# A tiny load ahead of the first big one in a streaming row-sum kernel

## The chip, the cores and the metric

The kernel runs on one core of one Trainium2 chip. The metric is the device time of one execution in microseconds (us); lower is better. The time given is the median of several runs of the same program. A profile of one execution shows what each engine did: DVE is the vector engine, ACT the scalar engine, POOL the GpSimd engine, and SP the sync engine, which here only issues DMA transfers (SPq in the profile is its instruction queue).

## The reference

```python
def setup_inputs():
    batch, seq, dim = 32, 512, 1024
    return {"x": np.random.randn(batch, seq, dim).astype(np.float32)}

def reference(x):
    relu_x = np.maximum(x, 0)
    return np.sum(relu_x, axis=-1).astype(np.float32)
```

The input is 16384 rows of 1024 float32 values, 67.1 MB in all. Each row is clamped below at zero and summed; the output is 16384 sums, 64 KB.

## The kernel before, in words

The rows are seen as 128 partitions of 128 rows. A block is 16 rows on each of the 128 partitions, 8 MB, so there are eight blocks. Block 0 is taken from the first 2048 rows (its source is contiguous, 64 KB for each partition); blocks 1 to 7 share the other 14336 rows, 112 for each partition, so their 64 KB runs lie 448 KB apart.

Three buffers `io0` to `io2`, each 64 KB for each partition, take the blocks in turn. All transfers are issued by SP, in the order of the program, and go into one DMA queue. `load` (L97 to L104, the transfer itself at L99) issues a transfer with a semaphore of its own; from block 3 on it first waits on the DVE semaphore until the block that held the buffer before has been summed. The seven blocks 0 to 6 are whole transfers of 8 MB. The last block is cut into six: 8 rows, 4 rows, then 4 rows in four pieces (1164, 642, 120 and 122 KB), so that little work is left when the last bytes land. The two last pieces go to small tiles `piece0` and `piece1`.

ACT clamps a block in place (`clamp`, L117) once its load's semaphore stands at 16; DVE then sums it (`total`, L125). In blocks 5 and 6 and in the tail single rows are clamped and summed by one instruction, on ACT (`act_row`, L132) or on DVE (`dve_row`, L140, and the last one at L224). Sums go to the tile `res`. Three stores (`store`, L109 waits for ACT, L110 issues the transfer and waits for DVE) write `res` to the output: block 0's sums, the rest but two columns, and the last two columns. At the very end SP clears the semaphores (L46) and waits until the stores have landed (L47).

The program has an opening block, in which the engines do their own setup (POOL writes four constants), and then a body. `open_without_barrier` takes the barrier out of the opening block and moves the first `EARLY` instructions of SP's body to the front of SP's part of the opening block; it asserts that they are transfers:

```python
    loads = [i for i in body if i.engine == SP][:n_loads]
    for i in loads:
        assert isinstance(i, mybir.InstDMACopy)
        body.remove(i)
    at = next(n for n, i in enumerate(opening) if i.engine == SP)
    opening[at:at] = loads
```

With `EARLY = 1` block 0's load is SP's first instruction. SP then branches to the body and issues the loads of blocks 1 and 2, without a wait.

Of the kernel before, what the change touches and what calls it, by code (L numbers as in the profile page):

```python
# [4 lines left out]
F32 = mybir.dt.float32  # L5
RELU = mybir.ActivationFunctionType.Relu
MAX, ADD = mybir.AluOpType.max, mybir.AluOpType.add
P = 128
# [5 lines left out]
TWO = [[16], [16], [16], [8, 8], [8, 8], [7, 7], []]  # L14
# [5 lines left out]
TAIL = [8, 4]  # L20
START_PIECE, END_PIECE = 280, 260
PIECES = [240, 244]

EARLY = 1


def kernel(tc: tile.TileContext, x: bass.AP, out: bass.AP):
    nc = tc.nc
    sems = Semaphores(tc)

    tc.close()
    tc.compile()
    nc.cur_bb = nc.bb_map[tc.start_bb_name]
    body = nc.cur_bb.bb.instructions
    ends = list(body)
    body.clear()
    n_stores = relu_sum(nc, sems, x, out)
    body.extend(ends)


    nc.cur_bb = nc.bb_map[tc.start_bb_name + "_end"]
    nc.cur_bb.bb.instructions.clear()
    nums = sorted(s.num for s in (*sems.loads, sems.act, sems.dve))
    cleared = range(nums[0], nums[-1] + 1)
    assert len(cleared) == len(nums)
    nc.sync.sem_clear(cleared)  # L46
    nc.sync.wait_ge(sems.stored, 16 * n_stores).then_inc(sems.stored, -16 * n_stores)  # L47
    open_without_barrier(tc, EARLY)


class Semaphores:
    def __init__(self, tc: tile.TileContext):
        n = len(TWO) + len(TAIL) + 2 + len(PIECES)
        self.loads = [tc.alloc_semaphore(f"load{i}") for i in range(n)]
        self.act = tc.alloc_semaphore("act")
        self.dve = tc.alloc_semaphore("dve")
        self.stored = tc.alloc_semaphore("stored")


def relu_sum(nc, sems: Semaphores, x: bass.AP, out: bass.AP):  # L60
    x_flat = x.flatten_outer_dims()
# [4 lines left out]
    assert sum(TAIL) == ROWS - 4 and START_PIECE + END_PIECE + sum(PIECES) == D  # L66

    bufs = [nc.alloc_sbuf_tensor(f"io{i}", [P, ROWS, D], F32) for i in range(NBUF)]
    res = nc.alloc_sbuf_tensor("res", [P, NT], F32)

    extra = len(PIECES) + 1
# [18 lines left out]
    def sums(m, n):  # L90
        if m < ROWS:
            return of[:, m : m + n], res[:, m : m + n]
        return ov[:, m - ROWS : m - ROWS + n], res[:, m : m + n]
# [3 lines left out]
    def load(dst, src, after=None):  # L97
        nonlocal n_load
        dma = nc.sync.dma_start(out=dst, in_=src)  # L99
        if after:  # L100
            dma.wait_op(sems.dve, after[1], "sem-ge")
        dma.then_inc(sems.loads[n_load], 16)
        n_load += 1
        return sems.loads[n_load - 1]  # L104

    def store(m, n, act, dve):
        nonlocal n_store
        dst, src = sums(m, n)
        nc.sync.wait_ge(sems.act, act)  # L109
        nc.sync.dma_start(out=dst, in_=src).wait_op(sems.dve, dve, "sem-ge").then_inc(  # L110
            sems.stored, 16
        )
        n_store += 1
# [24 lines left out]
    def dve_row(ap, accum_out, loaded):  # L138
# [12 lines left out]
        i.then_inc(sems.dve, 1)  # L151
        n_dve += 1

    freed = []
    m = 0
    for j in range(NB):
# [58 lines left out]

    store(0, ROWS, *freed[0])
    store(ROWS, NT - ROWS - 2, sums_act, sums_dve)

# [17 lines left out]
def open_without_barrier(tc: tile.TileContext, n_loads: int):  # L238

    SP = mybir.EngineType.SP
    blocks = tc.nc.main_func.blocks
    opening = blocks[0].instructions
    body = next(b for b in blocks if b.name == tc.start_bb_name).instructions
    for i in list(opening):
        if isinstance(i, (mybir.InstDrain, mybir.InstEventSemaphore)):
            opening.remove(i)
# [6 lines that stand above are left out]
# [30 lines left out]
```

## Time and profile before

| | |
|---|---|
| median of 3 runs | 161.29 us (161.19 to 161.3) |
| span of the profiled execution, first to last instruction | 159.6 us |
| median less span, work around the program's instructions | 1.7 us |
| DVE busy | 117.6 us (74%) |
| ACT busy | 104.2 us (65%) |
| POOL busy | 0.2 us |
| read from memory, mean rate over the span | 67.11 MB, 421 GB/s |
| packets of the one DMA queue | 2304 |
| SP's first load issued | 0.00 us |
| ACT's first clamp starts | 21.87 us |

How to read it: the page gives no time of the profiled execution other than its span, so the span is set beside the median of the timed runs; what lies around the span is the difference. All times inside the profile count from the first instruction. The packet records of the trace give, for every DMA packet, when it started, how long it took and its size; a load of one block is 128 packets of 64 KB, eight for each of 16 DMA engines.

### The profile page before, as it was taken

How to read it: one execution, taken by the hardware profiler on the slowest of the kernel's cores; microseconds unless marked ns; L12 is line 12 of the kernel's file. 1: busy time of each engine (PE TensorE's matmuls, PEld its weight loads, DVE VectorE, ACT ScalarE, POOL GpSimd, SP SyncE). 2: the span in 40 equal slices, each digit the busy share in tenths (PEclk: the TensorE clock that was granted, in tenths of full speed). 3: DMA queues.
4: the chain of work that ended last, by engine and by line, in shares of the span. 5: the costliest groups of instructions: out<-in, count | busy, mean ns of one | idle time of the engine just before them, and what ended most of it. 6: DMA issues, size and time to landing. Idle time of an engine off the chain costs nothing.

```text
span 159.6 us, 120 instructions
## 1 busy us (share of the span) xinstructions
DVE 117.6 (74%) x43; ACT 104.2 (65%) x50; POOL 0.2 (0%) x4
## 2 busy tenths in 40 slices
DVE  0000000009999499994999999999999999999986
ACT  3000059990699708996099951999329993499995
POOL 0000000000000000000000000000000000000000
DMA  7996996996997999979979969969969969798993
GB/s 279 509 526 263 526 526 263 526 509 279 526 476 312 526 394 394 526 345 443 526 328 460 526 263 526 526 263 526 509 279 526 493 296 526 337 452 382 418 412 119
DMA packets 2304, 67.18 MB, mean 421 GB/s; under 512 B 640, under 2 KB 896, under 8 KB 1024
## 3 DMA queue, kind: packets, MB, share of 16 engines
q1 hardware_dynamic: 2304, 67.18, 98.0%
HBM read 67.11 MB, written 0.07 MB: 421 GB/s over the span
## 4 chain that ended last, share of the span: by engine, by line
DMA 43%; DVE 34%; ACT 17%; another core or an unknown queue 3%; SPq 1%; issue 0%
DMA io<-in_x_dram 43%; DVE res L125 32%; ACT io L117 17%; DVE io L140 1%; SPq L99 1%; DVE piece L224 0%; DVE piece L140 0%
## 5 line engine op out<-in xcount | busy, mean ns | idle before, releaser
L125 DVE TENSOR_REDUCE res<-io 128x8 f32<-128x8192 f32 (+2 forms) x9 | 101.1, 11287 | 40.0 <-ACT io L117 40.0
L117 ACT ACTIVATE io<-io 128x8192 f32<-128x8192 f32 (+2 forms) x9 | 81.7, 9110 | 47.7 <-DMA io<-in_x_dram 47.7
L132 ACT ACTIVATE io<-io 128x1024 f32<-128x1024 f32 x20 | 20.9, 1045 | 6.0 <-DMA io<-in_x_dram 6.0
L140 DVE TENSOR_SCALAR_CACHE_REDUCE io<-io 128x1024 f32<-128x1024 f32 (+2 forms) x15 | 15.8, 1110 | 0.5 <-DMA io<-in_x_dram 0.4
L132 ACT ACTIVATION_READ_ACCUMULATOR io<-io 128x1 f32 x20 | 3.8, 188 | 0.0
L117 ACT ACT_TABLE_LOAD x1 | 1.3, 1283 | 0.1
L140 DVE DVE_READ_ACCUMULATOR io<-io 128x1 f32 x15 | 1.2, 82 | 0.0
L224 DVE TENSOR_SCALAR_CACHE_REDUCE piece<-piece 128x247 f32<-128x247 f32 x1 | 0.4, 410 | 0.0
L140 DVE TENSOR_SCALAR_CACHE_REDUCE piece<-piece 128x240 f32<-128x240 f32 x1 | 0.4, 397 | 0.0
L269 POOL MEMSET const-bfloat16-1.0<- 128x1 bf16 x1 | 0.1, 101 | 0.0
L269 POOL MEMSET const-uint8-127<- 128x1 uint8 x1 | 0.1, 101 | 0.0
L269 POOL MEMSET const-float32-0.0<- 128x1 f32 x1 | 0.1, 98 | 0.2 <-issue 0.2
L269 POOL MEMSET const-float32-1.0<- 128x1 f32 x1 | 0.1, 98 | 0.0
L224 DVE DVE_READ_ACCUMULATOR piece<-piece 128x1 f32 x1 | 0.1, 83 | 0.0
L140 DVE DVE_READ_ACCUMULATOR piece<-piece 128x1 f32 x1 | 0.1, 82 | 0.0
## 6 DMA issues: line engine op xcount, KB each, us to landing
io<-in_x_dram SPq DMA_DIRECT2D x1, 4096.0 KB, 21.6
io<-in_x_dram SPq DMA_DIRECT2D x1, 2048.0 KB, 26.1
io<-in_x_dram SPq DMA_DIRECT2D x1, 1164.0 KB, 28.4
io<-in_x_dram SPq DMA_DIRECT2D x1, 642.0 KB, 29.5
piece<-in_x_dram SPq DMA_DIRECT2D x1, 122.0 KB, 29.2
piece<-in_x_dram SPq DMA_DIRECT2D x1, 120.0 KB, 29.4
io<-in_x_dram SPq DMA_DIRECT2D x7, 26.9
out_dram<-res SPq DMA_DIRECT2D x1, 55.0 KB, 1.6
```

Source lines behind the costliest of these rows:

```text
L99: dma = nc.sync.dma_start(out=dst, in_=src)
L117: i = nc.scalar.activation(out=ap, in_=ap, func=RELU)
L125: nc.vector.tensor_reduce(out=res[:, m : m + n], in_=ap, axis=mybir.AxisListType.X, op=ADD).wait_op(sems.act, n_act, "sem-ge").then_inc(se ...
L132: i = nc.scalar.activation(out=ap, in_=ap, func=RELU, accum_out=accum_out)
L140: i = nc.vector.tensor_scalar(out=ap, in0=ap, scalar1=0.0, scalar2=None, op0=MAX, op1=ADD, accum_out=accum_out,)
L224: nc.vector.tensor_scalar(out=last[:, :], in0=last[:, :], scalar1=0.0, scalar2=None, op0=MAX, op1=ADD, accum_out=res[:, NT - 2 : NT - 1],) ...
L269: nc = _bacc.Bacc("TRN2", target_bir_lowering=False, num_devices=1)
```

## The change

`EARLY` becomes 2 and a new load is put ahead of all others: 8 bytes for each of 16 rows, from the first 16 rows of `x`, into 16 partitions of a new scratch tile `woken`. It has a semaphore of its own. It becomes SP's first instruction and block 0's load the second; both stand ahead of the branch to the body. Nothing reads `woken`; SP waits for the new semaphore once, just ahead of the first store.

```diff
-EARLY = 1
+EARLY = 2
...
-        n = len(TWO) + len(TAIL) + 2 + len(PIECES)
+        n = 1 + len(TWO) + len(TAIL) + 2 + len(PIECES)
...
     bufs = [nc.alloc_sbuf_tensor(f"io{i}", [P, ROWS, D], F32) for i in range(NBUF)]
+    woken = nc.alloc_sbuf_tensor("woken", [P, 2], F32)
     res = nc.alloc_sbuf_tensor("res", [P, NT], F32)
...
+    wake = load(woken[:16, :], x_flat[:16, :2])
     freed = []
...
+    nc.sync.wait_ge(wake, 16)
     store(0, ROWS, *freed[0])
     store(ROWS, NT - ROWS - 2, sums_act, sums_dve)
```

In the built program the scratch tile moves `res`, `piece0` and `piece1` up by 32 bytes in each partition; the three buffers stay where they were. No instruction of ACT, DVE or POOL is added, removed or moved.

## The prediction

> **What bounds the kernel now.** I read the chain that ended last first. From the page and, below it, the end of the same chain in order of time (start, length, what):
>
> ```profile
> DMA 43%; DVE 34%; ACT 17%; another core or an unknown queue 3%; SPq 1%; issue 0%
> ...
> 126.91 28.43 DMA io<-in_x_dram
> 155.34 0.02 issue
> 155.37 2.02 DVE io L140 x6
> 157.39 0.33 DVE piece L140 x2
> 157.72 0.02 issue
> 157.74 0.42 DVE piece L224 x2
> ```
>
> The chain passes through ACT and DVE in the middle, which could be read as a compute bound. The waits and ACT's timeline (start, length, instruction, idle time before it and what ended that) say otherwise:
>
> ```profile
> ACT io L117 <- DMA io<-in_x_dram: 47.7, 6, 20.5
> ...
> 21.87 13.86 ACT L117 ACTIVATE io<-io 128x16384 f32<-128x16384 f32 x1 [20.47 <-DMA io<-in_x_dram]
> 41.19 13.86 ACT L117 ACTIVATE io<-io 128x16384 f32<-128x16384 f32 x1 [5.46 <-DMA io<-in_x_dram]
> 60.55 13.86 ACT L117 ACTIVATE io<-io 128x16384 f32<-128x16384 f32 x1 [5.50 <-DMA io<-in_x_dram]
> 79.90 13.95 ACT L117 ACTIVATE io<-io 128x8192 f32<-128x8192 f32 x2 [5.50 <-DMA io<-in_x_dram]
> ```
>
> ACT starts each block when it lands and then idles some 5.4 us; blocks land every 19.35 us, (79.90 - 41.19)/2. The next view is the queue:
>
> ```profile
> q1 hardware_dynamic: 2304, 67.18, 98.0%
> ...
> SPq L99 <- DVE res L125: 123.3, 5, 51.7
> ```
>
> The queue's packets fill 98.0% of sixteen engines' span. SP does wait for DVE before it issues later blocks, which puts DVE into the chain, but block 3's load is issued at 53.0 us while block 2 lands only at 60.5 us: 7.5 us of stock in the queue. The packet records show the same on every engine: chained by end and start, 64 KB packets take 2.418 us each, with breaks of at most 4 ns from the first packet to the last of the input. So the end is where the slowest DMA engine's first packet ends, plus a fixed amount of streaming, plus a DVE tail that starts on landings. What shifts the stream by d shifts the end by d.
>
> **The start, which is all the change touches.** At 19.35 us a block the first could land at 19.35; ACT starts at 21.87, so the start costs 2.5 us. SP's early timeline:
>
> ```profile
> 0.00 0.86 SPq L99 DMA_DIRECT2D io<-in_x_dram  x2
> ...
> 0.12 1.28 ACT L117 ACT_TABLE_LOAD   x1
> ...
> L99 SPq DMA_DIRECT2D io<-in_x_dram x11: 327/383/442, 0.0 to 127.4; - x11
> ```
>
> The first issue lasts 0.383 us, the second starts at 0.433. By the packet records the sixteen first packets start between 1.014 and 1.810 us (five by 1.05, the last three at 1.52, 1.72 and 1.81) and take 2.50 to 3.27 us instead of 2.418. Start plus excess is the moment from which an engine streams at full rate: 1.55 to 2.17 us. The slowest starts at 1.397, takes 3.187 and ends at 4.584; its offset stays to the end of the input. From its 2.17 us, 0.3 us more lie between a block's last packet and its semaphore (eight packets end at 21.52, the last landing is 21.85).
>
> For comparison, the only transfer onto an empty queue later: the last store is issued at 158.188 to 158.521, its packets start at 159.014 (0.83 us after the issue began, 0.49 after it ended), and the sixteen semaphore packets lie within 0.15 us. The first load needs 0.63 us from issue end to the first packet and 0.80 us from the first engine to the last. So 0.14 us of latency and some 0.65 us of spread may be a first-use cost. Or they may belong to reading 64 KB runs from memory on sixteen engines at once, which a store from on-chip memory does not do. The trace of before cannot tell these apart, and the forecast hangs on it.
>
> **Part by part.**
>
> - *One more issue ahead of block 0.* Price: one issue (0.327 to 0.383 us by the row above) and the 0.04 us gap to the next, so 0.37 to 0.42; nothing hides it, since SP's first instruction starts the span. The program's first issue is the longer one, so I take 0.42.
> - *What the small load gives back.* Lower end nothing: the latency and the spread of block 0 repeat. Next bound 0.14 us: the common latency, if only that is first use. I take half of this, 0.07. The far bound is the rival below.
> - *The small load's own packets.* One 8-byte packet and one semaphore packet for each engine; such packets take 7 to 9 ns in the last store, so 0.02 us, inside the latency of block 0: nothing on the path. If block 0 had to wait until they were confirmed, see the second rival.
> - *Blocks 1 and 2 are issued 0.4 us later*: covered by block 0's 19 us of streaming. The queue's stock of 7.5 us moves along with landings.
> - *The wait ahead of the first store*: one semaphore instruction, 17 ns at L109, on SP at 128.9 us, after the last load's issue. Behind it stand only the stores; SP waits until 156.5 for the second one anyway, 27 us of cover. The new semaphore was raised 125 us earlier.
> - *32 bytes of shift of `res` and the pieces, one more semaphore in the range that is cleared* (a single instruction, 58 ns at the end): nothing. The bound is the pieces' packets, 45 ns each and sixteen for each engine; a tenth more is 0.07 us, kept in the range.
> - *The tail*: DVE's last 2.8 us follow landings and move with them.
>
> Sum: 0.42 - 0.07 = +0.35 us, 161.29 + 0.35 = 161.64 (span 159.6 to 160.0, with the same 1.7 us around it). Ends of this case: 0.37 - 0.14 = +0.23, and 0.42 + 0.07 + 0.1 for a longer issue of block 0 behind a busy issuer (second issues last 0.43 us and more) = +0.6; so 161.5 to 161.9.
>
> The Trainium skill speaks against the change: "DMA: Bandwidth & Descriptors", section "Rules for kernel authors", says that many small transfers should be coalesced, since under 64 KB one pays mostly overhead. By that rule the 128 bytes are pure loss; the row prices the loss at one issue. The same page, "Latency and other measured facts", gives about 0.8 us as the least round trip to memory; put on the path whole, it would make the sum +1.2 us instead of +0.35. No row shows a later packet waiting for such a trip.
>
> **The rivals.**
>
> *The small load takes the slow start on itself (faster).* Place: the sixteen engines between 1.0 and 2.2 us. If the spread is each engine's first use, the small load spends it while SP is still issuing block 0. Its packets start as late as block 0's did (to 1.81), and block 0's follow at once; without excess the slowest ends at 1.81 + 2.42 = 4.23 instead of 4.58: -0.35 us, 160.94. If even the wake is shorter, the floor is the second issue's end, 0.42 + 0.38, plus 0.49 of latency, plus 2.42 = 3.71: -0.87, 160.42. For it: the spread of 0.80 us against 0.15, and the first five engines starting together while eleven trail. Against it: the engine that ends last is not one that starts late; it started at 1.397 and lost 0.77 us inside its packet, and the one that started last lost only 0.08. That looks like sixteen readers held up in common rather than engines asleep, and a read of 8 bytes each does not repeat that load. It decides from the point where the slowest first packet ends before 4.26 us.
>
> *Issue and gain cancel (no change).* The late engines start as before at up to 1.81, the early ones no longer at 1.01 but near 1.3, and the excess stays up to 0.85: 1.3 + 0.85 + 2.42 = 4.57 against 4.58. 161.3, within 0.2% (0.32 us, about what a measurement of this kernel can tell from no change).
>
> *Block 0 waits for the small load's confirmation (slower by more).* Between the last packet and the last semaphore of a load lie 0.3 to 0.4 us. On top of 0.42 that is +0.8: 162.1. Against it: semaphore packets stand between all blocks, and no engine pauses there for more than 4 ns.
>
> That the change doesn't do what it says is excluded by the built order: SP's list begins with the 16x2 load, then block 0, then the branch. Whether the engines are any readier for it is the first rival.
>
> **How the numbers follow.** The forecast (serial cost) 0.46, of which 0.04 falls under +0.32; the fast rival 0.35, of which 0.02 is too small to count; no change 0.14; confirmation 0.05. So faster 0.33, within 0.2% 0.20, slower 0.47. The range must reach into the fast rival: from 160.7, a little beyond the middle of that rival's two prices (160.94 and 160.42), to 161.95, just over the forecast's upper end; left out are the confirmation case and the rest of the fast one, under 2 in 10. The forecast's own range is 161.5 to 161.9.
>
> **What would show it.** Right: SP's first issue 0.33 to 0.38 us, block 0's at about 0.42; first 64 KB packets starting at 1.3 us or later with the old spread; ACT's first clamp at 22.2 instead of 21.87; all later rows shifted by the same 0.35; blocks still 19.35 us apart. Wrong: a first clamp at or before 21.6, with first packets that start within 0.2 us of each other or take close to 2.42 us (fast rival); a clamp at 21.8 to 21.95 (cancelled); or block distances other than 19.35, which would mean that the change reached beyond the start.

## The result, and the profile after

The changed kernel is slower by about what one issue costs: 161.49 us (161.42 to 161.66, 11 runs) against 161.13 us (160.93 to 161.30, 11 runs), a ratio of 1.0025 with a 95% interval of 1.0017 to 1.0034, that is +0.27 to +0.55 us around a difference of 0.36 us. The three runs that were known before are among the eleven.

The page and the end of the chain in order of time, of the changed kernel:

```profile
span 160.1 us, 121 instructions
...
q1 hardware_dynamic: 2336, 67.18, 97.7%
...
DMA 43%; DVE 34%; ACT 17%; another core or an unknown queue 3%; SPq 1%; issue 0%
```

```profile
127.36 28.42 DMA io<-in_x_dram
155.78 0.02 issue
155.81 1.59 DVE io L141 x4
...
158.20 0.42 DVE piece L227 x2
```

There is one instruction more and 32 packets more (a data packet and a semaphore packet for each engine); the chain's shares are the same in whole per cent. The last stretch begins 0.46 us later than before (127.36 against 126.91) and is as long. Everything from the first block on is 0.43 to 0.47 us later, as SP's and ACT's timelines show (start, length, instruction, idle time before it):

```profile
0.00 0.39 SPq L100 DMA_DIRECT2D woken<-in_x_dram  x1
0.44 1.36 SPq L100 DMA_DIRECT2D io<-in_x_dram  x3
```

```profile
22.30 13.86 ACT L118 ACTIVATE io<-io 128x16384 f32<-128x16384 f32 x1 [20.90 <-DMA io<-in_x_dram]
41.66 13.86 ACT L118 ACTIVATE io<-io 128x16384 f32<-128x16384 f32 x1 [5.50 <-DMA io<-in_x_dram]
61.01 13.86 ACT L118 ACTIVATE io<-io 128x16384 f32<-128x16384 f32 x1 [5.49 <-DMA io<-in_x_dram]
80.36 13.95 ACT L118 ACTIVATE io<-io 128x8192 f32<-128x8192 f32 x2 [5.49 <-DMA io<-in_x_dram]
```

Block 0's load is issued at 0.44 instead of 0.00 and the first clamp starts at 22.30 instead of 21.87. Blocks stay (80.36 - 41.66)/2 = 19.35 us apart: the change did not reach beyond the start. SP's wait for DVE before later blocks is the same too, which says that the stock of work in the queue moved along:

```profile
SPq L100 <- DVE res L126: 123.3, 5, 51.6
...
SPq L110 <- ACT io L133: 28.4, 2, 27.2
```

The packet records tell what the small load did on the engines. Its sixteen 8-byte packets start between 0.994 and 1.187 us, a spread of 0.19, and take 7 ns. So the first transfer of the program reached all engines almost at once, by 1.2 us. Block 0's packets come behind them: they start between 1.479 and 2.021 us, closer together than before (0.54 against 0.80 us), and last 2.67 to 3.42 us instead of 2.418. The slowest first packet ends at 5.061 us, before at 4.584; that is 0.477 us later, and block 0's issue ends 0.471 later (0.854 against 0.383). For the engine that decides nothing was gained.

### The profile page after: what moved, and what is told of

Read it like the earlier page. It is cut to its first block, busy times and chain, and to the rows that moved or that the text cites. A ratio compares the mean times of both kernels' runs of the same rounds, so it can differ in the third digit from the quotient of the medians.

```text
span 160.1 us, 121 instructions
## 1 busy us (share of the span) xinstructions
DVE 117.6 (73%) x43; ACT 104.2 (65%) x50; POOL 0.2 (0%) x4
## 4 chain that ended last, share of the span: by engine, by line
DMA 43%; DVE 34%; ACT 17%; another core or an unknown queue 3%; SPq 1%; issue 0%
DMA io<-in_x_dram 43%; DVE res L126 32%; ACT io L118 17%; DVE io L141 1%; SPq L100 1%; DVE piece L227 0%; DVE piece L141 0%
```

## The experiments

Two theories stood against each other: that the issue ahead of block 0 is the whole price and nothing comes back, and that the small load takes over some first-use cost of the engines. Later runs asked where the slow start comes from. The diffs with a `wake` line stand against the changed kernel, the others against the kernel before; lines left out are marked by `...`.

**The small load behind block 0.**

```diff
-    wake = load(woken[:16, :], x_flat[:16, :2])
...
         loaded = load(buf[:, :, :], rows(m, ROWS), j >= NBUF and freed[j - NBUF])
+        if j == 0:
+            wake = load(woken[:16, :], x_flat[:16, :2])
```

> The small load is kept, but issued second, right behind block 0's load and ahead of the branch. Theory (the issue ahead of block 0 is the whole price): block 0's issue is back at 0.00, the first clamp at 21.9 us as before, the time within 0.1 us of before (161.1). Rival (the small load's packets, its semaphore or the shifted addresses cost wherever it stands): +0.3 to +0.45 us as with the change.

Measured: 161.04 us against 161.05, ratio 1.0 (0.9992 to 1.0009). Everything else of the change is in this kernel (scratch tile, shifted addresses, semaphore, the wait ahead of the first store), and it costs nothing that can be seen (by the interval, under 0.15 us either way). From its timeline:

```profile
0.00 0.38 SPq L100 DMA_DIRECT2D io<-in_x_dram  x1
...
0.43 0.42 SPq L100 DMA_DIRECT2D woken<-in_x_dram  x1
...
21.89 13.86 ACT L118 ACTIVATE io<-io 128x16384 f32<-128x16384 f32 x1 [20.48 <-DMA io<-in_x_dram]
```

The same issue, 0.42 us long, stands on the same queue; only block 0 is no longer behind it.

**A delay in place of the small load.**

```diff
-EARLY = 1
+DELAY = 4
+EARLY = 1 + DELAY
...
+    for _ in range(DELAY):
+        nc.sync.sem_clear(range(sems.spare.num, sems.spare.num + 1))
     freed = []
```

> No small load; in its place four clears of an unused semaphore stand ahead of block 0's load on SP, which take some time d (0.25 to 0.45 us, to be read from block 0's issue start). Theory (nothing is given back): first clamp at 21.87 + d, the time of before + d. Rival (the small load gives something back, say 0.07 to 0.14 us of first-use latency, or the spread of the engines): this kernel is slower, for the same d, than the change by what is given back; packets would start later after the issue's end than the 0.63 us of the change.

Measured: 161.30 us against 161.05, ratio 1.0014 (1.0005 to 1.0022). The four clears take d = 0.251 us, and the time rises by 0.25. From its timelines, SP's and ACT's:

```profile
0.25 1.32 SPq L101 DMA_DIRECT2D io<-in_x_dram  x3
```

```profile
22.16 13.86 ACT L119 ACTIVATE io<-io 128x16384 f32<-128x16384 f32 x1 [20.75 <-DMA io<-in_x_dram]
```

The clamp moved by 0.29, a little over d. By the packet records the first packet of block 0 starts 0.629 us after the issue's end here, 0.625 with the small load ahead and 0.631 in the kernel before. The slowest engine reaches full rate 2.22 us after the issue began here and 2.20 with the small load. By both measures the small load does no more for block 0 than an idle wait does.

**Two small loads.**

```diff
-EARLY = 2
+EARLY = 3
...
     wake = load(woken[:16, :], x_flat[:16, :2])
+    wake2 = load(woken2[:16, :], x_flat[:16, :2])
```

> Two small loads of the same shape ahead of block 0. Theory: each costs one issue and a gap, so block 0's issue starts at 0.85 to 0.9 us and the time is before + 0.75 to 0.9 us. Rival (a cost that comes once, for whatever stands first): before + 0.36, as with one.

Measured: 162.07 us against 161.05, ratio 1.0062 (1.0049 to 1.0074), that is +0.79 to +1.19.

```profile
0.00 0.84 SPq L101 DMA_DIRECT2D woken<-in_x_dram  x2
0.88 1.37 SPq L101 DMA_DIRECT2D io<-in_x_dram  x3
```

```profile
22.81 13.86 ACT L119 ACTIVATE io<-io 128x16384 f32<-128x16384 f32 x1 [21.41 <-DMA io<-in_x_dram]
```

Block 0 is issued at 0.88, twice the 0.44 of one small load, and the first clamp starts 0.94 us later than before. A cost that comes once is out: +0.36 lies far below the interval. The middle of the measurement, +1.02, lies above the 0.9 that was expected, but 0.88 is inside the interval.

**The small load on one partition.**

```diff
-    wake = load(woken[:16, :], x_flat[:16, :2])
+    wake = load(woken[:1, :], x_flat[:1, :2])
```

> The small load reads 8 bytes into one partition, so it has one data packet on one engine. Theory (the price is the issue on SP, whatever is moved): block 0's issue at 0.40 to 0.45 us, before + 0.3 to 0.45 us. Rival (packets on all sixteen engines ahead of block 0 carry part of the price): before + 0.2 us or less. A second rival (touching all sixteen engines gives something back): clearly more than the change, before + 0.55 or above.

Measured: 161.45 us against 161.05, ratio 1.0022 (1.0013 to 1.0031).

```profile
0.00 0.34 SPq L100 DMA_DIRECT2D woken<-in_x_dram  x1
0.40 1.31 SPq L100 DMA_DIRECT2D io<-in_x_dram  x3
```

One packet on one engine costs what sixteen cost, as far as the intervals tell. This run also answers the confirmation rival. In the changed kernel the last semaphore of the small load rises at 1.460 us and block 0's first packet starts at 1.479, which looks like a wait. Here the semaphore stands at 16 at 1.172 us, and block 0's first packets still start from 1.398 us on: 0.637 after the issue's end, as everywhere else.

**The small load from ACT's queue.**

```diff
-    wake = load(woken[:16, :], x_flat[:16, :2])
+    wake = sems.loads[-1]
+    nc.scalar.dma_start(out=woken[:16, :], in_=x_flat[:16, :2]).then_inc(wake, 16)
```

with `EARLY = 1`, so that block 0 is SP's first instruction again.

> The same small load, issued as ACT's first instruction on ACT's queue, so that block 0's load stands first on SP as before. Theory (the small load has no use, only its place ahead of block 0 costs): block 0's issue at 0.00, first clamp at 21.8 to 22.0, time within 0.1 us of before. Rival (touching the engines early helps where it is free): first packets with less spread or nearer to 2.42 us, 0.2 us faster or more. Second rival (a second queue disturbs the start): 0.1 to 0.4 us slower.

Measured: 161.04 us against 161.06, ratio 1.0001 (0.9993 to 1.001). Where the load is free it gives nothing:

```profile
0.00 1.33 SPq L100 DMA_DIRECT2D io<-in_x_dram  x3
0.12 0.38 ACTq L156 DMA_DIRECT2D woken<-in_x_dram  x1
```

It is issued 0.12 us after block 0, and by the packet records its sixteen packets run only between 4.118 and 4.671 us, when the engines' first packets of block 0 have ended. No engine was touched early, so this run is no test of an early touch; it shows that a small load on a second queue does no harm.

**Block 0 in two parts, one row first.**

```diff
-        loaded = load(buf[:, :, :], rows(m, ROWS), j >= NBUF and freed[j - NBUF])
+        if j == 0:
+            first = load(buf[:, :FIRST, :], rows(0, FIRST))
+            loaded = load(buf[:, FIRST:, :], rows(FIRST, ROWS - FIRST))
+            nc.scalar.wait_ge(first, 16)
+        else:
+            loaded = load(buf[:, :, :], rows(m, ROWS), j >= NBUF and freed[j - NBUF])
```

with `FIRST = 1` here, 4 and 8 in the two kernels after it. ACT's wait for the first part is long over when block 0 has landed.

> No small load. Block 0 is loaded as 1 row for each partition (packets of 4 KB) and then 15 rows; useful bytes stand where the change put a scratch load. The second issue is covered by the first part's 1.2 us of packets (8 x 0.15 us for each engine). Theory (the hold-up of the start belongs to sixteen engines starting to read at once, whatever the packets): engines reach full rate at 1.5 to 2.2 us as before, first clamp at 21.8 to 22.0, time within 0.15 us of before. Rival (it belongs to the first 64 KB packet, and small packets start the engines well): small packets start within 0.2 us of each other and run at 0.15 us each, full rate from about 1.2 us, 0.4 to 0.9 us faster than before.

Measured: 161.48 us against 161.06, ratio 1.0022 (1.0013 to 1.0031): slower, which neither theory expected.

```profile
22.50 13.86 ACT L118 ACTIVATE io<-io 128x16384 f32<-128x16384 f32 x1 [16.80 <-DMA io<-in_x_dram]
```

By the packet records the first 4 KB packets start within 0.33 us of each other, but take 0.19 to 1.35 us, where later ones take 0.159. So packets of 4 KB are held up at the start as well; those of 8 bytes were not. On one engine the eight small packets end only at 3.99 us, on most at 2.9 to 3.2. The slowest engine ends block 0 at 22.101 us, before at 21.495. That is 0.61 us later, and the first clamp is 0.63 later, so in the profiled execution (161.60 us, above the median) the slowest engine accounts for the whole loss. Why small first packets leave one engine so late is open.

**Four rows first.**

> As the last one, with 4 rows first (packets of 16 KB) and then 12. Theory: within 0.1 us of before. Rival (packet size decides): a gain between that of one row first and none.

Measured: 160.99 us against 161.06, ratio 0.9995 (0.9986 to 1.0003). The first 16 KB packets take 0.83 to 1.42 us, steady ones 0.611. No difference that this can tell.

**Eight rows first.**

> Block 0 loaded as 8 rows (packets of 32 KB) and then 8. With 16 KB packets first the time stood at 0.9995 of before, an interval that holds 1. Theory (the start's hold-up does not depend on the packet): within 0.1 us of before. Rival (a smaller first packet helps a little): 0.1 us faster or more.

Measured: 160.98 us against 161.12, ratio 0.999 (0.998 to 1.0001). The median is where the rival wanted it, but the interval just holds 1; a gain of a tenth of a microsecond is not shown. Neither split is shown to beat the kernel before.

**Another source pitch.**

```diff
-    xf = x_flat[:N1].rearrange("(p m) d -> p m d", p=P)
-    xv = x_flat[N1:].rearrange("(p m) d -> p m d", p=P)
+    xf = x_flat[NL:].rearrange("(p m) d -> p m d", p=P)
+    xv = x_flat[:NL].rearrange("(p m) d -> p m d", p=P)
...
-    store(0, ROWS, *freed[0])
-    store(ROWS, NT - ROWS - 2, sums_act, sums_dve)
+    store(0, NT - ROWS, *freed[NB - 1])
+    store(NT - ROWS, ROWS - 2, sums_act, sums_dve)
```

The views of rows and sums are exchanged to match, so the last block is now the contiguous one.

> Blocks 0 to 6 come from the first 14336 rows, so block 0's 64 KB runs lie 448 KB apart as those of the other blocks do, and the last block is the contiguous one; the first store waits for seven blocks instead of one. Theory (the hold-up does not depend on how the first block's runs lie in memory): first packets start from 1.0 us with a spread of 0.5 to 0.8, latest full-rate moment 2.0 to 2.3 us, first clamp 21.8 to 22.0. Rival (the runs of block 0 collide because they lie 64 KB apart): latest full-rate moment moves by 0.2 us or more, and the first clamp with it.

Measured: 161.12 us against 161.06, ratio 1.0003 (0.9994 to 1.0011). The first clamp starts at 21.82 us. The start is as slow with runs 448 KB apart: packets from 1.005 to 2.019 us, the latest engine at full rate at 2.13 us. How far apart the first block's runs lie, 64 or 448 KB, is not the reason.

**A queue that runs empty once.**

```diff
+        if j == 1:
+            nc.sync.wait_ge(loaded, 16)
         buf = bufs[j % NBUF]
```

> No small load. SP waits until block 0 has landed before it issues block 1, so the queue runs empty once after all sixteen engines have read 512 KB each. Theory (the slow start belongs to every start of sixteen readers on an empty queue, not to first use): block 1's packets start 0.9 to 1.1 us after its issue began, with a spread of 0.4 to 0.8 us and a length of 2.5 to 3.3 us; the engines are at full rate some 1.5 to 2.2 us after the issue began, and the time is before + 2.0 to 2.5 us (the start's 1.8 to 2.2, the 0.3 us from a last packet to its semaphore, and SP's wait). Rival (first use): block 1's packets start 0.8 to 0.9 us after the issue, within 0.2 us of each other, and take 2.42 us; before + 1.2 to 1.5 us.

Measured: 163.55 us against 161.12, ratio 1.0147 (1.0131 to 1.0164), that is +2.1 to +2.6. ACT's timeline and SP's waits:

```profile
21.91 13.86 ACT L117 ACTIVATE io<-io 128x16384 f32<-128x16384 f32 x1 [20.51 <-DMA io<-in_x_dram]
43.79 13.86 ACT L117 ACTIVATE io<-io 128x16384 f32<-128x16384 f32 x1 [8.02 <-DMA io<-in_x_dram]
63.14 13.86 ACT L117 ACTIVATE io<-io 128x16384 f32<-128x16384 f32 x1 [5.49 <-DMA io<-in_x_dram]
```

```profile
SPq L99 <- DMA io<-in_x_dram: 21.5, 1, 21.5
```

ACT idles 8.02 us before block 1, 2.5 more than before the next block. Block 1's load is issued at 21.903 us, when all engines have read for 20 us. Its packets start between 22.864 and 23.812, 0.95 us apart, and take 2.42 to 3.53 us; the slowest ends at 26.534. That is the start of the program over again, with a spread and a longest packet somewhat above what was expected. First use is out as the reason of the slow start.

The table puts the starts side by side, from the packet records. "Full rate" is the end of the slowest first packet less 2.418 us, counted from the start of that load's issue.

| load that meets an idle queue (or only small loads) | issue starts at | issue end to first packet | issue start to full rate, slowest | median against before |
|---|---|---|---|---|
| before, block 0 | 0.000 | 0.631 | 2.17 | |
| small load from ACT | 0.000 | 0.645 | 2.25 | -0.02 |
| delay | 0.251 | 0.629 | 2.22 | +0.25 |
| small load, one partition | 0.397 | 0.637 | 2.30 | +0.40 |
| the change | 0.444 | 0.625 | 2.20 | +0.36 |
| two small loads | 0.883 | 0.625 | 2.23 | +1.02 |
| drained queue, block 1 | 21.903 | 0.628 | 2.21 | |

The third column agrees within 0.02 us and the fourth within 0.13; the last follows the second within its intervals.

## Why the prediction was right

The forecast was +0.35 us by a serial cost; the runs show +0.36. Point by point:

- *One more issue, 0.37 to 0.42.* Measured 0.389 for the issue and 0.055 to the next, 0.444. The step holds, but the term was too small. I took the row's least and middle length for its ends (its longest is 0.442) and a gap of 0.04, where my own reading, an issue of 0.383 us and the next at 0.433, had 0.05. Block 0's issue behind a busy issuer, kept as an upper end of +0.1, lasted 0.410 instead of 0.383.
- *Half of 0.14 us given back.* This term was wrong. I had compared a load's 0.63 us from issue end to first packet with a store's 0.49 and held the difference for a possible first-use cost. It is none: block 1 on the drained queue needs 0.628 too, and the one-packet load that comes first in its program needs 0.547. What comes back is 0 within the scatter of these rows, and the right sum is 0.44, or 0.47 with the longer issue of block 0. Both lie inside the measured interval, and the span of the profiled execution rose by 0.46. Two errors, an issue term too small and a gain that isn't there, shifted the forecast by some 0.1 us in the same direction; that the median stands at 0.36 all the same, right on the forecast, is partly luck.
- *The span beside the median.* I set 159.6 us of span against 161.29 and put 1.7 us around it. The profiled execution of the changed kernel gives both, 161.43 us and a span of 160.1, so some 1.35 lie around it. With that, the execution profiled before lasted about 160.97 us, near the fast end of its runs. The wrong offset did not touch the difference.
- *Small packets, wait, shift of addresses: nothing.* The small load behind block 0, ratio 1.0, shows it to within 0.15 us.
- *The fast rival.* The argument against it carried: the engine that ended last was not one that started late. The runs bear it out, since with engines touched by 1.2 us the slowest came to full rate 2.20 us after block 0's issue, and with untouched ones after 2.17 to 2.25. My sign for the forecast, the old spread, did not come: the first packets started within 0.54 us, and it was of no use, because the engine that comes to full rate last decides. The point in this rival's favour, 0.80 us of spread against a store's 0.15, compared a load with a store.
- *The cancelling rival.* It needed block 0's issue to be ready behind the late engines. But the hold-up is counted from block 0's own issue (2.17 to 2.30 us in every row of the table), not from a clock of the engines, so a later issue can't hide in it.
- *The confirmation rival.* Out by the run with one partition, and by the delay: the distance from issue end to first packet is the same with and without a small load.

The Trainium skill's "DMA: Bandwidth & Descriptors", section "Latency and other measured facts", gives about 0.6 us to the first byte for loads issued this way; the 0.63 us from issue end to first packet agrees, if it is counted from there, which the page does not say. The rule on coalescing small transfers got the sign right, but the price here was not the transfer's own overhead. It was the place of its issue: the same load costs 0.36 us ahead of block 0 and nothing that can be seen behind it.

What stays open is why sixteen engines that begin to read at once are held up until 2.2 us after the issue. It is not first use, not the pitch of the source, and a smaller first packet does not remove it. In every row of the table the issue of another load follows block 0's at once (block 1's on the drained queue); whether that plays a part no run shows.

## What to carry to other kernels

In a kernel bound by one stream of transfers, as this one is, expect to pay the whole time of each instruction that stands ahead of the first big transfer on its issuing engine; behind it, while the queue has work, the same instruction cost nothing that could be seen. Before paying for a warm-up, test whether the slow start is first use: let the queue run empty once in the middle and see if the start comes again. Compare like with like: a store's latency is no measure for a load's, so no term of the sum should rest on it.

## What the runs showed of the hardware

Loads of 64 KB packets on sixteen engines start slowly on an empty queue, at the program's start and again after 20 us of reading: 0.63 us from issue end to the first packet, packets spread over 0.5 to 1.1 us, the first ones up to 1.1 us longer than the steady 2.418 us, and the slowest engine at full rate some 2.2 us after the issue began. Packets of 8 bytes start within 0.19 us and take 7 ns; packets of 4 KB start within 0.33 us but take up to 1.35 instead of 0.159. An engine's delay at the start stays with it: in the kernel before, with packets chained by end and start, the engine whose first packet ends last, at 4.584 us, also ends its last 64 KB packet last, at 137.535, and the sixteen engines lie 0.62 us apart at the first and 0.60 at the second. As a program's first instruction, the issue of a load takes SP 0.34 us for 8 bytes on one partition, 0.39 for 8 bytes on each of sixteen, and 0.38 for 8 MB.
